# Tokens and gates in one product, and the two chunks of a group by turns in the halves of TensorE's columns, in a hybrid streaming encoder layer

## The chip, the cores and the metric

The kernel runs on one core of one Trainium2 chip. The metric is the device time of one execution in microseconds. The profile names the engines PE (matrix products), PEld (loads of the stationary operand, which overlap PE), DVE (vector), ACT (scalar), POOL and SP (which issues DMAs).

## What is computed

One inference step of one layer over 2048 prompt frames and 32 frames of a running stream. Three mixers work on parts of one input projection; the change touches the second and the third:

```python
hn = rmsnorm(x, norm1); proj = hn @ w_in
ya = rmsnorm(rg_lru(causal_conv(pa_x))) * gelu(pa_g)      # 256 channels
yb = rwkv7_mix(pb)                                        # 6 heads x 64, a recurrence over time
yc = mlstm_mix(pc)                                        # 6 heads x 64
# mlstm_mix, in chunks of 64 frames:
xact = silu(causal_conv(xc)); q = xact @ wq; k = xact @ wk
gates = concat([q, k, vc]) @ w_if + b_if                  # 12 columns: i_pre and logf of 6 heads
num = w_inter * (q @ C0) + (q @ k.T * exp(log_w - m)) @ v
h = num / max(|den|, exp(-m))
C_new = w0_end * C0 + (w_end * k).T @ v
# then
x = x + concat([ya, yb, yc]) @ w_out
x = x + (silu(g) * u) @ w_ffn_out                         # g, u = halves of rmsnorm(x) @ w_ffn_in
y = rmsnorm(x)
```

## The kernel before

The frames stand in four blocks of 512 (the last one 544, in two of 272, with the sample frames at its end). `inproj` makes the input projection of a block, `phase2` the output projection and the feed-forward part. Both use fp32r products of a high and a low part, 128x128 stationary by 512 or 272 columns, which the profile shows as writers of `pj`. The mixers run on groups of 128 frames, 16 of the prompt and one shorter group of the sample. A group has two chunks of 64 frames (`nch` is 2). Tiles named `rw` in the profile belong to the second mixer, tiles named `ml` to the third and the first.

Nothing is issued in the order in which the functions run. A recorder keeps every instruction with what it depends on. `order` then plays all engines forward with estimated durations (`cost`) and writes down an order for each engine: evacuations first, then weights, then mixers in bursts limited by a debt, and the `pj` products as filling (`Recorder.order`). Every instruction has the line of the recorder's call, L339, so tiles and shapes tell the groups apart. PE executes in the order written down, apart from what the hardware overlaps.

Four places matter.

`rwkv_c` ends with `yps`: for each chunk and each of three pairs of heads one product `Un,Hr` (stationary 128x64, 128 columns) and two products `SV,Fr` (stationary 128x64, 64 columns) that accumulate on it. Chunk 0 writes partitions 0 to 63, chunk 1 partitions 64 to 127, and thus the other half of the array's columns. All of chunk 0 is written ahead of chunk 1.

`mlstm` makes the gates `gp` by six products of `xa` and `v` with `wga` (128x128 by 12 columns), and later brings `v` and `k` to tokens by six transposes (`tokens`, into `vt` and `kt`, against the identity). `KW`, the weighted `k`, is read from PSUM by DVE.

`mlstm` makes its output `Op` by 12 products `R,QS` (128x64 by 65 columns), six for each chunk, chunk inside the loop. Those of chunk 0 need only the state at the group's start, those of chunk 1 the state `Rs[1]` after chunk 0.

`wq` and `wk` lie in SBUF for the whole time as a part of `smw`; the prompt groups don't read them.

Of the kernel before, what the change touches and what calls it, by code (L numbers as in the profile page):

```python
# [54 lines left out]
SMW = {}  # L55
# [7 lines left out]
NSMW = _n  # L63
NSMS = SMW["wif"][0]

# [80 lines left out]
class Op:  # L146
    __slots__ = ("eng", "fn", "args", "kw", "dur", "lat", "prio", "succ", "need", "ready", "start", "end", "idx", "rank", "mode")


class Recorder:  # L150
# [3 lines left out]
    def __init__(self, nc):  # L154
        self.ops = []
        self.level = MIX
        self.mem = {}
        self.masks = {}
        self.engines = {n: RecEngine(self, n, e) for n, e in (
            ("pe", nc.tensor), ("dve", nc.vector), ("act", nc.scalar), ("pool", nc.gpsimd), ("dma", nc.sync))}  # L160
# [41 lines left out]
    def add(self, eng, fn, name, args, kw):  # L202
# [13 lines left out]
        o.mode = tile_mode(ins[0]) if eng == "pe" else None  # L216
        deps = set()
        for a in ins:
# [28 lines left out]
    def order(self):  # L247
# [6 lines left out]
        debt, burst = 0.0, False  # L254
        mode = None
        for o in self.ops:
# [5 lines left out]
        while left:  # L262
# [36 lines left out]
            if best == "pe":  # L299
                if o.mode != mode:  # L300
                    when += DRAIN
                    mode = o.mode
                if o.prio == 1:
                    debt = max(debt, 0.0) + o.dur
                    burst = True
                elif o.prio == 2:
                    debt -= o.dur * RATE
                    burst = False
# [56 lines left out]
def cost(eng, name, out, ins, kw):  # L365

    n = 1
# [7 lines left out]
    if eng == "pe":  # L375
        if name == "transpose":
            return max(n, int(out.ap[0][1])) * 0.85, 196.0
        st = ins[0]
        if st.dtype == F32R:
            return max(n, 256) / 2.25 + 4.0, 196.0  # L380
        m = 1
        for _, c in list(st.ap)[1:]:
            m *= int(c)
        if m == 32:
            return max(38.0, 0.7 * n), 196.0
        if m == 64:
            return (92.0 if n < 70 else 1.15 * n), 196.0
        return 4.0 * max(m, n) / 2.4 + 4.0, 196.0
# [50 lines left out]
def hybrid_kernel(ctx, tc, A, O, cfg):  # L439
# [69 lines left out]

    wga = cp.tile([128, 6, 12], F32, name="wga")  # L510
    bones = cp.tile([128, 128], F32R, name="bones")
# [6 lines left out]
    histc = [cp.tile([128, 3, 3], F32, name=f"histc{i}") for i in range(2)]  # L518
    hlru = [cp.tile([128, 2], F32, name=f"hlru{i}") for i in range(2)]

    def setup():
# [26 lines left out]
        V.tensor_scalar(out=nsp, in0=nsp, scalar1=-4.0, scalar2=None, op0=ALU.mult)  # L548

        V.tensor_scalar(out=W("wq"), in0=W("wq"), scalar1=0.5, scalar2=None, op0=ALU.mult)  # L550
        V.tensor_scalar(out=W("wk"), in0=W("wk"), scalar1=0.5 / 8, scalar2=None, op0=ALU.mult)
        V.tensor_scalar(out=wif[:, 36:72], in0=wif[:, 36:72], scalar1=8.0, scalar2=None, op0=ALU.mult)


        V.tensor_copy(wga[:, 3:6, :], wif[:, 72:108].rearrange("p (a g) -> p a g", a=3))
        pg_ = mlp.tile([128, 512], F32, tag="ml", name="pg")
        wts = []
        for wn, o in (("wq", 0), ("wk", 36)):
            pt = rwp.tile([128, 512], F32, tag="rw", name="pt")[:, :384].rearrange("p (a t) -> p a t", a=3)
            for p in range(3):  # L560
                PE.transpose(pt[:, p, :], W(wn, 128 * p, 128 * p + 128), ident)
            wt = rws.tile([128, 3, 128], F32, tag="c" if o else "ta", name="wt")
            S.activation(wt, pt, AF.Copy)
            wts.append(wt)
            for p in range(3):
                PE.matmul(pg_[:, o + 12 * p:o + 12 * p + 12], wt[:, p, :], wif[:, o + 12 * p:o + 12 * p + 12], start=True, stop=True)
# [536 lines left out]
    def rwkv_c(Zf, BKU, SVt, UV, eL, g, bv, n_real, nch, st, col):  # L1103
# [53 lines left out]
        yps = rps("yps")[:, :384].rearrange("p (q t) -> p q t", q=6)  # L1157
        for c in range(nch):
            cs = slice(64 * c, 64 * c + 64)
            for p in range(3):  # L1160
                PE.matmul(yps[cs, 2 * p:2 * p + 2, :], Hr[:, p, c, 64:128], UN[c][:, p, :, :], start=True, stop=False)
                for j in range(2):
                    PE.matmul(yps[cs, 2 * p + j, :], Fr[:, p, c, 1, j, :], SVt[:, p, c, j, :],
                              start=False, stop=(j == 1))
# [37 lines left out]

    ml_state = [None, None]

    def mlstm_init(st):
# [16 lines left out]
    def mlstm_out(st, dst, dst_m):  # L1222
        R, mr = ml_state[st]
        if st == 0:
            ps = mps("mem")[:, :198].rearrange("p (a t) -> p a t", a=3)
            for p in range(3):
                for j, hs in halves():
                    PE.matmul(ps[hs, p, 0:65], W("wk", 128 * p + 64 * j, 128 * p + 64 * j + 64)[hs], R[hs, p, j, 0:65],
                              start=True, stop=True)
            for j, hs in halves():  # L1230
                S.activation(R[hs, :, j, 0:65], ps[hs, :, 0:65], AF.Copy)
        for j, hs in halves():
            SY.dma_start(dst[hs], R[hs, :, j, 0:65])
        SY.dma_start(dst_m, mr[:, 0:1])

    def mlstm(src, n_real, nch, st, col):
# [14 lines left out]
        k = t3("KW") if st else xa  # L1251
        for w_, dst in (((W("wq").rearrange("p (a e) -> p a e", a=3), None), (W("wk").rearrange("p (a e) -> p a e", a=3), k))
                        if st else ((wqk, None),)):
            ps = mps("qk")[:, :3 * n].rearrange("p (a t) -> p a t", a=3)
            for p in range(3):
                PE.matmul(ps[:, p, :], w_[:, p, :], xa[:, p, :], start=True, stop=True)
            if dst is not None:
                S.activation(dst, ps, AF.Copy)
            else:
                for j, hs in halves():  # L1260
                    S.activation(QM[hs, :, j, :n], ps[hs], AF.Copy)
        gp = mps("gp")
        for i_, x in enumerate((xa, v)):
            for p in range(3):
                PE.matmul(gp[:n, 0:12], x[:, p, :], wga[:, 3 * i_ + p, :], start=(i_ + p == 0), stop=(i_ + p == 3))
        gt = ml([128, 12], "gt")
        V.tensor_tensor(out=gt[:n], in0=gp[:n, 0:12], in1=bif[:n], op=ALU.add)
        f = gt[:n, 6:12]
# [7 lines left out]
        if n_real < n:  # L1276
# [13 lines left out]
                             op0=ALU.add, op1=ALU.max)  # L1290
        R, mr = ml_state[st]
        mu3 = mu.rearrange("p (c t) -> p c t", c=nch)
# [33 lines left out]
        for j, hs in halves():  # L1326
            oh = slice(64, 128) if j == 0 else slice(0, 64)
            S.activation(WI[hs], wl[oh], AF.Exp)
        QS = ml([128, 3, 2, 2, 64], "QS")[:, :, :nch]
        for j, hs in halves():  # L1330
# [4 lines left out]
            for c in range(nch):  # L1335
# [3 lines left out]
                            in1=ch(WI)[hs], op=ALU.mult)  # L1339
        D4 = ch(Dm)  # L1340
        W4 = ch(WI)
        Rs = [R]
        for c in range(nch):
            Rs.append(ml([128, 3, 2, 66], "R", bufs=3))
            G.memset(Rs[-1][:, :, :, 64:65], 1.0)
        vt = mps("vt")[:, :384].rearrange("p (a t) -> p a t", a=3)
        tokens(vt, v, n)
        for c in range(nch):
            for j in range(2):
                S.activation(Rs[c][64 * (1 - j):64 * (1 - j) + 64, :, j, 0:64],  # L1350
                             vt[64 * c:64 * c + 64, :, 64 * j:64 * j + 64], AF.Copy)
        kt = mps("kt")[:, :384].rearrange("p (a t) -> p a t", a=3)
        tokens(kt, k, n)
        KW = ml([128, 2, 3, 64], "KW")
        for c in range(nch):
            for j in range(2):
                oh = slice(64 * (1 - j), 64 * (1 - j) + 64)
                V.tensor_tensor(out=KW[oh, c], in0=kt[64 * c:64 * c + 64, :, 64 * j:64 * j + 64],
                                in1=bc(D4[oh, :, c, 63:64], [64, 3, 64]), op=ALU.mult)
        for c in range(nch):  # L1360
# [7 lines left out]
            for j, hs in halves():  # L1368
                V.tensor_tensor(out=Rn[hs, :, j, 0:65], in0=Rc[hs, :, j, 0:65],
                                in1=bc(W4[hs, :, c, 63:64], [64, 3, 65]), op=ALU.mult)  # L1370
                V.tensor_tensor(out=Rn[hs, :, j, 0:65], in0=Rn[hs, :, j, 0:65], in1=up[hs, :, 0:65], op=ALU.add)
        ml_state[st] = (Rs[nch], mr2)
        Op = mps("Op")[:, :396].rearrange("p (q t) -> p q t", q=6)
        for p in range(3):
            for j in range(2):
                for c in range(nch):
                    PE.matmul(Op[64 * c:64 * c + 64, 2 * p + j, 0:65], QS[:, p, c, j, :], Rs[c][:, p, j, 0:65],
                              start=True, stop=True)

        tm = mps("tm")  # L1380
# [314 lines left out]
```

## Time and profile before

| | |
|---|---|
| median of 3 runs | 2756.22 us (2750.87 to 2759.62) |
| profiled execution, its own time | 2758.22 us |
| its span in the profile | 2756.4 us |
| PE busy | 2699.3 us (98%) |
| DVE busy | 2170.4 us (79%) |
| ACT busy | 1290.2 us (47%) |
| mean granted clock of PE | 0.992 of full speed |

The profiled execution takes 1.8 us more than its span. A busy share is an average over the span; products overlap in PE's pipeline, so what a product costs is read from the start of one to the start of the next, not from its duration.

### The profile page before, as it was taken

To read this page: it belongs to the slowest core of one execution; us is meant where nothing else is said; L and a number is where in the kernel's file an instruction comes from. 1 tells how busy PE (TensorE), PEld (TensorE's weight loads), DVE (VectorE), ACT (ScalarE), POOL (GpSimd) and SP (SyncE) were. 2 spreads that over 40 slices of the span, in tenths; PEclk is the share of its full clock that TensorE was granted. 3 is DMA by queue.
4 is the path that set the end of the run, shared out by engine and by line. 5 is a ranking of instruction groups with operands and counts; after the bars stand their busy time and mean duration, and the time that the engine had idled before them with its cause. 6 is when DMAs were issued, how large, how long until landed. Compare 5 with 4: busy or idle time off the path is not lost.

```text
span 2756.4 us, 47320 instructions
## 1 busy us (share of the span) xinstructions
PE 2699.3 (98%) x17021; PEld 2324.8 (84%) x17021; DVE 2170.4 (79%) x6107; ACT 1290.2 (47%) x2847; POOL 44.3 (2%) x171
## 2 busy tenths in 40 slices
PE   8999999999999999999999999999999998999998
PEld 7888887999878888887888888788888888999997
DVE  6788879888897898979888898989888555545556
ACT  5565655656554454455444444644443333222223
POOL 0000000000000000000000000000000000000000
PEclk9999999999999999999999999999999999999999
DMA  6453543544433333344333333353333334232232
GB/s 240 144 173 116 175 139 119 166 128 119 126 89 101 97 92 110 88 124 153 98 107 97 105 95 105 105 161 98 85 99 89 96 110 147 85 93 85 85 93 79
DMA packets 235955, 317.86 MB, mean 115 GB/s; under 512 B 63848, under 2 KB 147736, under 8 KB 235592
## 3 DMA queue, kind: packets, MB, share of 16 engines
q1 hardware_dynamic: 189860, 300.74, 35.5%
q10 hardware_dynamic: 45860, 14.10, 2.4%
q8 instruction: 134, 2.20, 0.3%
q14 instruction: 101, 0.83, 0.1%
HBM read 268.50 MB, written 46.27 MB: 114 GB/s over the span
## 4 chain that ended last, share of the span: by engine, by line
PE 71%; DVE 20%; DMA 4%; ACT 3%; issue 2%; ACTq 0%; SPq 0%; DVEq 0%
PE pj L339 61%; PE rw L339 7%; DVE wl L339 4%; PE ml L339 4%; DVE stg L339 2%; DVE utmp L339 1%; DVE x L339 1%; DVE Z L339 1%; DVE al L339 1%; DVE hl L339 1%; DMA sq<-ymix 1%; DVE Fr L339 1%; ACT wh L339 1%; DVE Dm L339 1%; DVE acc L339 1%
## 5 line engine op out<-in xcount | busy, mean ns | idle before, releaser
L339 PE MATMUL pj<-ah,wh 128*128 128x512 f32 (+1 forms) x2560 | 894.2, 357 | 7.8 <-DVE x L339 6.5
L339 PE MATMUL pj<-al,wh 128*128 128x512 f32 (+1 forms) x2560 | 893.9, 356 | 0.2 <-DVE al L339 0.2
L339 PE MATMUL pj<-ah,wl 128*128 128x512 f32 (+1 forms) x2560 | 825.3, 354 | 1.0 <-DVE wl L339 1.0
L339 ACT ACTIVATE wh<-raw 128x1024 fp32r<-128x1024 f32 (+2 forms) x444 | 383.0, 863 | 735.3 <-PE pj L339 600.2
L339 PEld LDWEIGHTS pj<-ah,wh 128*128 128x128 f32 x2560 | 484.0, 189 | 73.0 <-DVE x L339 6.7
L339 PEld LDWEIGHTS pj<-al,wh 128*128 128x128 f32 x2560 | 486.7, 190 | 61.3 <-DVE al L339 0.8
L339 PEld LDWEIGHTS pj<-ah,wl 128*128 128x128 f32 x2560 | 454.2, 189 | 66.4 <-DVE wl L339 2.1
L339 DVE TENSOR_TENSOR wl<-raw,wh 128x1024 fp32r<-128x1024 f32 (+2 forms) x444 | 432.0, 974 | 62.3 <-ACT wh L339 61.0
L339 PE MATMUL pj<-hh,wh 128*128 128x512 f32 (+1 forms) x856 | 297.3, 359 | 3.4 <-ACT hh L339 3.4
L339 PE MATMUL pj<-hl,wh 128*128 128x512 f32 (+1 forms) x856 | 299.5, 357 | 0.4 <-DVE hl L339 0.4
L339 PE MATMUL pj<-hh,wl 128*128 128x512 f32 (+1 forms) x856 | 278.6, 355 | 0.0
L339 DVE TENSOR_TENSOR x<-x,pj 128x512 f32<-128x512 f32 (+1 forms) x280 | 158.5, 582 | 109.3 <-PE pj L339 102.3
L339 PEld LDWEIGHTS pj<-hh,wh 128*128 128x128 f32 x856 | 160.8, 189 | 27.0 <-ACT hh L339 4.8
L339 PEld LDWEIGHTS pj<-hl,wh 128*128 128x128 f32 x856 | 161.9, 190 | 24.1 <-DVE hl L339 3.3
L339 PE MATMUL pj<-ah,hh 128*128 128x512 f32 (+1 forms) x480 | 168.0, 357 | 7.5 <-ACT hh L339 7.4
L339 PEld LDWEIGHTS pj<-hh,wl 128*128 128x128 f32 x856 | 152.5, 189 | 22.3
L339 PE MATMUL pj<-al,hh 128*128 128x512 f32 (+1 forms) x480 | 168.2, 358 | 0.0
L339 PE MATMUL pj<-ah,hl 128*128 128x512 f32 (+1 forms) x480 | 154.4, 354 | 0.0
L339 DVE TENSOR_TENSOR cbuf<-pj,acc 128x512 f32<-128x512 f32 (+1 forms) x110 | 62.5, 585 | 87.0 <-PE pj L339 85.3
L339 DVE TENSOR_TENSOR stg<-stg,pj 128x512 f32<-128x512 f32 (+1 forms) x110 | 62.4, 583 | 85.6 <-PE pj L339 84.7
L339 DVE TENSOR_TENSOR utmp<-Z,BK 96x60 f32<-96x60 f32 (+27 forms) x527 | 106.1, 201 | 9.9 <-DMA BK<-tb 5.1
L339 DVE TENSOR_TENSOR Z<-Z,utmp 96x60 f32<-96x60 f32 (+27 forms) x527 | 106.1, 201 | 4.9
(343 smaller groups left out, 3896.8 us busy)
## 6 DMA issues: line engine op xcount, KB each, us to landing
raw<-in_w_ffn_in SPq DMA_DIRECT2D x176, 512.0 KB
raw<-in_w_ffn_out SPq DMA_DIRECT2D x128, 256.0 KB
raw<-in_w_in SPq DMA_DIRECT2D x96, 256.0 KB
raw<-in_w_in SPq DMA_DIRECT2D x48, 512.0 KB
spill<-stg SPq DMA_DIRECT2D x72, 256.0 KB
raw<-in_w_out SPq DMA_DIRECT2D x32, 512.0 KB
x<-in_xT SPq DMA_DIRECT2D x48, 256.0 KB
raw<-in_w_ffn_out SPq DMA_DIRECT2D x64, 192.0 KB
```

Source lines behind the costliest of these rows:

```text
L339: o.fn(*o.args, **o.kw)
```

## The change

Four edits. (1) In `yps` the loop over chunks goes inside, so that products of the two chunks alternate. (2) The gates and the tokens come out of one product: the new constant `iwg` holds, for each of six 128-row parts, the identity (128 columns) and beside it the part's gate weights (12 columns). `vt` and `kt` have 140 columns for each pair of heads; two reductions over the three parts and two additions make the gates; ACT copies the tokens of `k` to SBUF (`ks`), from which DVE makes `KW`. (3) All 12 products of `Op` wait in the order for the state after chunk 0 (`gate`). (4) The estimates that make the order change: a product with 64 stationary columns counts 4 + 0.85 ns a column, and one behind a product in the other half of the columns counts 7 ns. To make room for `iwg`, `wq` and `wk` are loaded twice, once in the setup and once ahead of the sample group.

```diff
@@ order
                 if o.mode != mode:
                     when += DRAIN
-                    mode = o.mode
+                    mode, side_ = o.mode, None
+
+                if mode[1] == 64 and side_ not in (None, o.col):
+                    o.dur = 7.0
+                    side_ = None
+                else:
+                    side_ = o.col
@@ cost
         if m == 64:
-            return (92.0 if n < 70 else 1.15 * n), 196.0
+            return 4.0 + 0.85 * n, 196.0
@@ constants and setup
-    wga = cp.tile([128, 6, 12], F32, name="wga")
+    iwg = cp.tile([128, 6, 140], F32, name="iwg")
+    wga = iwg[:, :, 128:140]
+    def load_qk(t):
+        o = SMW["wq"][0]
+        SY.dma_start(t, A["smalls"][:, o:o + 768])
+        V.tensor_scalar(out=t[:, 0:384], in0=t[:, 0:384], scalar1=0.5, scalar2=None, op0=ALU.mult)
+        V.tensor_scalar(out=t[:, 384:768], in0=t[:, 384:768], scalar1=0.5 / 8, scalar2=None, op0=ALU.mult)
+        S.activation(iwg[:, :, 0:128], bc(ident[:, None, :], [128, 6, 128]), AF.Copy)
@@ rwkv_c
-        for c in range(nch):
-            cs = slice(64 * c, 64 * c + 64)
-            for p in range(3):
-                PE.matmul(yps[cs, 2 * p:2 * p + 2, :], Hr[:, p, c, 64:128], UN[c][:, p, :, :], start=True, stop=False)
-                for j in range(2):
-                    PE.matmul(yps[cs, 2 * p + j, :], Fr[:, p, c, 1, j, :], SVt[:, p, c, j, :],
+        for p in range(3):
+            for c in range(nch):
+                PE.matmul(yps[64 * c:64 * c + 64, 2 * p:2 * p + 2, :], Hr[:, p, c, 64:128], UN[c][:, p, :, :],
+                          start=True, stop=False)
+            for j in range(2):
+                for c in range(nch):
+                    PE.matmul(yps[64 * c:64 * c + 64, 2 * p + j, :], Fr[:, p, c, 1, j, :], SVt[:, p, c, j, :],
                               start=False, stop=(j == 1))
@@ mlstm_out (ahead of the sample group)
+            wqk2[0] = ml([128, 768], "QS")
+            load_qk(wqk2[0])
@@ mlstm
-        gp = mps("gp")
-        for i_, x in enumerate((xa, v)):
-            for p in range(3):
-                PE.matmul(gp[:n, 0:12], x[:, p, :], wga[:, 3 * i_ + p, :], start=(i_ + p == 0), stop=(i_ + p == 3))
-        gt = ml([128, 12], "gt")
-        V.tensor_tensor(out=gt[:n], in0=gp[:n, 0:12], in1=bif[:n], op=ALU.add)
+        gt, ga = [ml([128, 12], f"gt{i}") for i in range(2)]
+        vt = mps("vt")[:, :420].rearrange("p (a t) -> p a t", a=3)
+        for p in range(3):
+            PE.matmul(vt[:n, p, :], v[:, p, :], iwg[:, 3 + p, :], start=True, stop=True)
+        V.tensor_reduce(out=gt[:n], in_=vt[:n, :, 128:140].rearrange("p a g -> p g a"), axis=AX.X, op=ALU.add)
+        V.tensor_tensor(out=gt[:n], in0=gt[:n], in1=bif[:n], op=ALU.add)
...
+        kt = mps("kt")[:, :420].rearrange("p (a t) -> p a t", a=3)
+        for p in range(3):
+            PE.matmul(kt[:n, p, :], xa[:, p, :], iwg[:, p, :], start=True, stop=True)
+        V.tensor_reduce(out=ga[:n], in_=kt[:n, :, 128:140].rearrange("p a g -> p g a"), axis=AX.X, op=ALU.add)
+        V.tensor_tensor(out=gt[:n], in0=gt[:n], in1=ga[:n], op=ALU.add)
...
+        S.activation(ks[:n], kt[:n, :, 0:128].rearrange("p a (j t) -> p a j t", j=2), AF.Copy)
...
-        vt = mps("vt")[:, :384].rearrange("p (a t) -> p a t", a=3)
-        tokens(vt, v, n)
...
-        kt = mps("kt")[:, :384].rearrange("p (a t) -> p a t", a=3)
-        tokens(kt, k, n)
...
-                V.tensor_tensor(out=KW[oh, c], in0=kt[64 * c:64 * c + 64, :, 64 * j:64 * j + 64],
+                    V.tensor_tensor(out=KW[oh, c], in0=ks[64 * c:64 * c + 64, :, j, :],
...
+            if c < nch - 1:
+                gate = len(rec.ops) - 1
+        rec.gate = gate if nch > 1 else None
         Op = mps("Op")[:, :396].rearrange("p (q t) -> p q t", q=6)
```

How the change moves instructions is shown on PE at three places. The first is `yps` of the first group: `Un0` and `Un1` are chunks 0 and 1. First before, then after.

```order
L339 MATMUL rw_0_170<-Un0_0_120,Hr_0_130 64x128
L339 MATMUL rw_0_170<-SV_0_155,Fr_0_129 64x64 x2
L339 MATMUL rw_0_170<-Un0_0_120,Hr_0_130 64x128
L339 MATMUL rw_0_170<-SV_0_155,Fr_0_129 64x64 x2
L339 MATMUL rw_0_170<-Un0_0_120,Hr_0_130 64x128
L339 MATMUL rw_0_170<-SV_0_155,Fr_0_129 64x64 x2
L339 MATMUL rw_0_170<-Un1_0_121,Hr_0_130 64x128
L339 MATMUL rw_0_170<-SV_0_155,Fr_0_129 64x64 x2
```

```order
L347 MATMUL rw_1_172<-UV_0_244,Fr_0_129 128x128 x3
L347 MATMUL rw_0_171<-Un0_0_120,Hr_0_130 64x128
L347 MATMUL rw_0_171<-Un1_0_121,Hr_0_130 64x128
L347 MATMUL rw_0_171<-SV_0_155,Fr_0_129 64x64 x4
L347 MATMUL rw_0_171<-Un0_0_120,Hr_0_130 64x128
L347 MATMUL rw_0_171<-Un1_0_121,Hr_0_130 64x128
```

The two chunks' products, nine in a row for each before, now stand by turns.

The second place is `Op` of the second group. `R_2_224` is the state at its start (chunk 0) and `R_0_222` the state after chunk 0; in the changed kernel these are `R_2_225` and `R_0_223`. Before, three products of chunk 0 are issued 37 rows earlier, in a block of their own, and the other nine stand here:

```order
L339 MATMUL pj_0_203<-ah6_0_190,hl1_0_144 128x512
L339 MATMUL ml_1_169<-R_2_224,QS_0_277 64x65
L339 MATMUL ml_1_169<-R_0_222,QS_0_277 64x65
L339 MATMUL ml_1_169<-R_2_224,QS_0_277 64x65
L339 MATMUL ml_1_169<-R_0_222,QS_0_277 64x65
L339 MATMUL ml_1_169<-R_2_224,QS_0_277 64x65
L339 MATMUL ml_1_169<-R_0_222,QS_0_277 64x65 x4
L339 MATMUL pj_0_203<-ah7_0_192,hh1_0_143 128x512
```

After the change (the first eight of the twelve):

```order
L347 MATMUL rw_0_171<-BK_0_168 64x64 x6
L347 MATMUL ml_0_169<-R_0_223,KW_0_279 64x65 x6
L347 MATMUL ml_1_170<-R_2_225,QS_0_267 64x65
L347 MATMUL ml_1_170<-R_0_223,QS_0_267 64x65
L347 MATMUL ml_1_170<-R_2_225,QS_0_267 64x65
L347 MATMUL ml_1_170<-R_0_223,QS_0_267 64x65
L347 MATMUL ml_1_170<-R_2_225,QS_0_267 64x65
L347 MATMUL ml_1_170<-R_0_223,QS_0_267 64x65
L347 MATMUL ml_1_170<-R_2_225,QS_0_267 64x65
L347 MATMUL ml_1_170<-R_0_223,QS_0_267 64x65
```

All twelve now stand in one block by turns. Over the whole program `Op` stands in 39 blocks before and in 19 after, for 17 groups.

The third place is the gates of the second group. Before:

```order
L339 MATMUL rw_0_170<-cl_0_128,bones_0_81 128x384
L339 MATMUL ml_0_168<-xi_0_264,wqk_0_82 128x128 x3
L339 MATMUL ml_1_169<-wga_0_80,xi_0_264 128x12 x5
L339 MATMUL rw_1_171<-cst_0_75,BK_0_241 128x128 x3
L339 MATMUL pj_0_203<-al7_0_193,hh1_0_143 128x512
```

After the change:

```order
L347 MATMUL rw_1_172<-yx_0_175,smw_0_77 128x128 x3
L347 MATMUL ml_1_170<-xi_0_264,wqk_0_82 128x128 x3
L347 MATMUL ml_0_169<-iwg_0_80,xi_0_264 128x140 x3
L347 MATMUL pj_2_206<-al1_0_179,hh2_0_151 128x512
L347 MATMUL pj_2_206<-ah1_0_178,hl2_0_152 128x512
```

Three products of 140 columns (those of `v`) stand where five of the six gate products were; the three of `xa` follow 20 rows later. The six transposes, which before stood further on, are gone.

## Rows read from the trace of the kernel before

**Rows 1.** Page, part 1: busy us, share of the span and instructions of each engine.
```profile
PE 2699.3 (98%) x17021; PEld 2324.8 (84%) x17021; DVE 2170.4 (79%) x6107; ACT 1290.2 (47%) x2847; POOL 44.3 (2%) x171
```

**Rows 2.** Windows: length, busy and count of PE, PEld, DVE, ACT, POOL, PEclk, DMA share, GB/s.
```profile
300.00:2100.00 1800.00, 1774.81 (x11069) 1489.16 (x11068) 1567.62 (x4701) 911.16 (x2109) 36.33 (x132) 0.99 0.38 113
2300.00:2500.00 200.00, 197.80 (x1559) 197.37 (x1560) 101.52 (x202) 58.56 (x92) 0.00 (x0) 0.99 0.30 95
```

**Rows 3.** Timeline of PE around one `yps`: start, us, engine, line, operation, count.
```profile
235.19 0.83 PE L339 MATMUL rw<-UV,Fr 128*128 128x128 f32 x6
235.95 0.43 PE L339 MATMUL rw<-Un,Hr 128*64 128x128 f32 x2
...
236.45 0.39 PE L339 MATMUL rw<-Un,Hr 128*64 128x128 f32 x2
...
236.90 0.38 PE L339 MATMUL rw<-Un,Hr 128*64 128x128 f32 x2
237.12 0.22 PE L339 MATMUL rw<-SV,Fr 128*64 128x64 f32 x1
237.13 0.32 PE L339 MATMUL rw<-Un,Hr 128*64 128x128 f32 x1
237.18 0.28 PE L339 MATMUL rw<-SV,Fr 128*64 128x64 f32 x2
237.29 0.27 PE L339 MATMUL rw<-Un,Hr 128*64 128x128 f32 x1
...
238.62 0.50 PE L339 MATMUL pj<-al,hh 128*128 128x512 f32 x1
238.96 0.40 PE L339 MATMUL pj<-ah,hl 128*128 128x512 f32 x1
239.19 0.39 PE L339 MATMUL pj<-ah,wh 128*128 128x512 f32 x1
```

**Rows 4.** Timeline of PE around the two blocks of one `Op`.
```profile
325.06 0.56 PE L339 MATMUL ml<-R,QS 128*64 128x65 f32 x6
325.56 0.50 PE L339 MATMUL pj<-ah,wh 128*128 128x512 f32 x1
...
335.50 0.40 PE L339 MATMUL pj<-ah,hl 128*128 128x512 f32 x1
335.82 0.92 PE L339 MATMUL ml<-R,QS 128*64 128x65 f32 x18
336.67 0.50 PE L339 MATMUL pj<-ah,hh 128*128 128x512 f32 x1
337.01 0.40 PE L339 MATMUL pj<-al,hh 128*128 128x512 f32 x1
```

**Rows 5.** Timeline of PE around one set of six transposes, one of six gate products.
```profile
1008.07 0.82 PE L339 MATMUL ml<-cst,xi 128*128 128x128 f32 x6
1008.64 0.47 PE L339 MATMUL pj<-hl,wh 128*128 128x512 f32 x1
1008.96 0.39 PE L339 MATMUL pj<-hh,wl 128*128 128x512 f32 x1
...
1071.83 0.83 PE L339 MATMUL ml<-xi,wqk 128*128 128x128 f32 x6
1072.50 1.41 PE L339 MATMUL ml<-wga,xi 128*128 128x12 f32 x12
1073.76 0.48 PE L339 MATMUL pj<-ah,wh 128*128 128x512 f32 x1
```

**Rows 6.** Groups of DVE and ACT by form: count, busy us, mean ns, idle before.
```profile
L339 DVE TENSOR_TENSOR gt<-ml,bif 128x12 f32<-128x12 f32 x16 | 2.7, 168 | 1.9 <-PE ml L339 1.6
L339 DVE TENSOR_REDUCE hmDm<-ml 128x6 f32<-128x384 f32 x16 | 8.8, 548 | 0.1
L339 ACT ACTIVATE g<-rw 128x384 f32<-128x384 f32 x16 | 7.8, 489 | 17.0 <-PE rw L339 6.7 <-DMA out_yT<-x 5.5 <-DMA BK<-tb 4.2
```

**Rows 7.** The chain that ended last, in time: start, us, what.
```profile
136.32 5.23 DMA xi<-spill
```

More of the change, by code (lines that the diff above doesn't have):

```diff
@@ L63 @@
 NSMW = _n
-NSMS = SMW["wif"][0]
+NSMS = SMW["wq"][0]
 def make_consts():
@@ L146 @@
 class Op:
-    __slots__ = ("eng", "fn", "args", "kw", "dur", "lat", "prio", "succ", "need", "ready", "start", "end", "idx", "rank", "mode")
+    __slots__ = ("eng", "fn", "args", "kw", "dur", "lat", "prio", "succ", "need", "ready", "start", "end", "idx", "rank", "mode", "col")
 class Recorder:
@@ L158, in __init__ @@
         self.masks = {}
+        self.gate = None
         self.engines = {n: RecEngine(self, n, e) for n, e in (
@@ L216, in add @@
         o.mode = tile_mode(ins[0]) if eng == "pe" else None
-        deps = set()
+        o.col = self.region(out)[1] if eng == "pe" else None
+        deps = set() if self.gate is None else {self.gate}
         for a in ins:
@@ L254, in order @@
         debt, burst = 0.0, False
-        mode = None
+        mode, side_ = None, None
         for o in self.ops:
@@ L548, in setup @@
         V.tensor_scalar(out=nsp, in0=nsp, scalar1=-4.0, scalar2=None, op0=ALU.mult)
-        V.tensor_scalar(out=W("wq"), in0=W("wq"), scalar1=0.5, scalar2=None, op0=ALU.mult)
-        V.tensor_scalar(out=W("wk"), in0=W("wk"), scalar1=0.5 / 8, scalar2=None, op0=ALU.mult)
+        wqk_ = rws.tile([128, 1024], F32, tag="BK", name="wqk_")[:, :768]
+        load_qk(wqk_)
         V.tensor_scalar(out=wif[:, 36:72], in0=wif[:, 36:72], scalar1=8.0, scalar2=None, op0=ALU.mult)
+        S.activation(iwg[:, :, 0:128], bc(ident[:, None, :], [128, 6, 128]), AF.Copy)
         V.tensor_copy(wga[:, 3:6, :], wif[:, 72:108].rearrange("p (a g) -> p a g", a=3))
@@ L557, in setup @@
         wts = []
-        for wn, o in (("wq", 0), ("wk", 36)):
+        for wn, o in ((0, 0), (384, 36)):
             pt = rwp.tile([128, 512], F32, tag="rw", name="pt")[:, :384].rearrange("p (a t) -> p a t", a=3)
             for p in range(3):
-                PE.transpose(pt[:, p, :], W(wn, 128 * p, 128 * p + 128), ident)
+                PE.transpose(pt[:, p, :], wqk_[:, wn + 128 * p:wn + 128 * p + 128], ident)
             wt = rws.tile([128, 3, 128], F32, tag="c" if o else "ta", name="wt")
@@ L1203, in hybrid_kernel @@
     ml_state = [None, None]
+    wqk2 = [None]
     def mlstm_init(st):
@@ L1227, in mlstm_out @@
                 for j, hs in halves():
-                    PE.matmul(ps[hs, p, 0:65], W("wk", 128 * p + 64 * j, 128 * p + 64 * j + 64)[hs], R[hs, p, j, 0:65],
+                    PE.matmul(ps[hs, p, 0:65], wqk2[0][hs, 384 + 128 * p + 64 * j:384 + 128 * p + 64 * j + 64], R[hs, p, j, 0:65],
                               start=True, stop=True)
@@ L1251, in mlstm @@
         k = t3("KW") if st else xa
-        for w_, dst in (((W("wq").rearrange("p (a e) -> p a e", a=3), None), (W("wk").rearrange("p (a e) -> p a e", a=3), k))
+        for w_, dst in (((wqk2[0][:, 0:384].rearrange("p (a e) -> p a e", a=3), None),
+                         (wqk2[0][:, 384:768].rearrange("p (a e) -> p a e", a=3), k))
                         if st else ((wqk, None),)):
@@ L1261, in mlstm @@
                     S.activation(QM[hs, :, j, :n], ps[hs], AF.Copy)
-        gp = mps("gp")
-        for i_, x in enumerate((xa, v)):
-            for p in range(3):
-                PE.matmul(gp[:n, 0:12], x[:, p, :], wga[:, 3 * i_ + p, :], start=(i_ + p == 0), stop=(i_ + p == 3))
-        gt = ml([128, 12], "gt")
-        V.tensor_tensor(out=gt[:n], in0=gp[:n, 0:12], in1=bif[:n], op=ALU.add)
+        R, mr = ml_state[st]
+        Rs = [R]
+        for c in range(nch):
+            Rs.append(ml([128, 3, 2, 66], "R", bufs=3))
+            G.memset(Rs[-1][:, :, :, 64:65], 1.0)
+        gt, ga = [ml([128, 12], f"gt{i}") for i in range(2)]
[4 more added lines that the diff above has]
+        V.tensor_tensor(out=gt[:n], in0=gt[:n], in1=bif[:n], op=ALU.add)
+        for c in range(nch):
+            for j in range(2):
+                S.activation(Rs[c][64 * (1 - j):64 * (1 - j) + 64, :, j, 0:64],
+                             vt[64 * c:64 * c + 64, :, 64 * j:64 * j + 64], AF.Copy)
+        kt = mps("kt")[:, :420].rearrange("p (a t) -> p a t", a=3)
[3 more added lines that the diff above has]
+        V.tensor_tensor(out=gt[:n], in0=gt[:n], in1=ga[:n], op=ALU.add)
+        if st:
+            kt = mps("kt")[:, :384].rearrange("p (a t) -> p a t", a=3)
+            tokens(kt, k, n)
+        ks = ml([128, 3, 2, 2, 64], "QS")
+        ks = (ks[:, :, 1] if st else ks.rearrange("p a c j t -> p (a c j t)")[:, :384].rearrange(
+            "p (a j t) -> p a j t", a=3, j=2))
+        S.activation(ks[:n], kt[:n, :, 0:128].rearrange("p a (j t) -> p a j t", j=2), AF.Copy)
         f = gt[:n, 6:12]
@@ L1290, in mlstm @@
                              op0=ALU.add, op1=ALU.max)
-        R, mr = ml_state[st]
         mu3 = mu.rearrange("p (c t) -> p c t", c=nch)
@@ L1328, in mlstm, with weigh @@
             S.activation(WI[hs], wl[oh], AF.Exp)
+        D4 = ch(Dm)
+        W4 = ch(WI)
+        KW = ml([128, 2, 3, 64], "KW")
+        def weigh():
+            for c in range(nch):
+                for j in range(2):
+                    oh = slice(64 * (1 - j), 64 * (1 - j) + 64)
+                    V.tensor_tensor(out=KW[oh, c], in0=ks[64 * c:64 * c + 64, :, j, :],
+                                    in1=bc(D4[oh, :, c, 63:64], [64, 3, 64]), op=ALU.mult)
+        if not st:
+            weigh()
         QS = ml([128, 3, 2, 2, 64], "QS")[:, :, :nch]
@@ L1339, in mlstm @@
                             in1=ch(WI)[hs], op=ALU.mult)
[L1340 to L1345, printed above, removed]
-        vt = mps("vt")[:, :384].rearrange("p (a t) -> p a t", a=3)
-        tokens(vt, v, n)
[L1348 to L1351, printed above, removed]
-        kt = mps("kt")[:, :384].rearrange("p (a t) -> p a t", a=3)
-        tokens(kt, k, n)
[L1354 to L1357, printed above, removed]
-                V.tensor_tensor(out=KW[oh, c], in0=kt[64 * c:64 * c + 64, :, 64 * j:64 * j + 64],
-                                in1=bc(D4[oh, :, c, 63:64], [64, 3, 64]), op=ALU.mult)
+        if st:
+            weigh()
         for c in range(nch):
@@ L1378, in mlstm @@
                               start=True, stop=True)
+        rec.gate = None
         tm = mps("tm")
```

## The prediction

> **What bounds the kernel now.** I read the page's part 1 first: PE is busy 2699.3 of 2756.4 us, DVE 2170.4, ACT 1290.2 [rows 1]. A busy PE alone says little, since products overlap in its pipeline. So I took the windows next. In the stretch in which mixers run beside the big products (300 to 2100 us) PE is idle for 1800.0 - 1774.8 = 25 us, DVE for 1800.0 - 1567.6 = 232 us, ACT for half of it, and the granted clock is 0.99. After the mixers (2300 to 2500) PE is idle for 2.2 us in 200 [rows 2]. The reader is to see that one engine is short of time nearly everywhere, at its full 2.4 GHz, and that DVE, at 87%, is next. The queue of `pj` products is never empty: in the order written down a whole `phase2` and part of another still stand behind the last mixer product, before and after the change. So a nanosecond that PE doesn't spend on a mixer product goes to a `pj` product, and the end comes earlier by as much, as long as DVE keeps up.
>
> What a product costs PE is then the time from its start to the next start, which the timeline of PE gives. A `pj` product of 512 columns takes 0.23 us (238.96 to 239.19) [rows 3]. An fp32 product shows as two records, two passes; a pass with 128 stationary rows and columns and 128 columns takes (1072.50 - 1071.83)/6 = 0.112 us [rows 5].
>
> **yps.** Before, it runs from 235.95 to 238.62, 2.67 us. One pair of heads of one chunk takes 236.90 - 236.45 = 0.45 us: two passes of `Un,Hr` at 0.11 and four of `SV,Fr` at 0.058 [rows 3]. That makes six times 0.45 for two chunks. Do two passes in different halves of the columns run at once? Two places show it. At the seam of the chunks, the only spot where neighbours lie in different halves, the first pass of chunk 1's `Un,Hr` starts at 237.13, 0.01 us behind a pass of chunk 0 and ahead of three passes of it that come earlier in the order (237.18 and after) [rows 3]. And the second block of an `Op`, 18 records whose first six products alternate, takes 336.67 - 335.82 = 0.85 us, where the first block, six records all of one chunk, takes 325.56 - 325.06 = 0.50 [rows 4]. With 0.058 a pass, six singles leave 0.50 - 0.35 = 0.15 for the change of tile mode; then 0.85 - 0.15 = 0.70 is 12 slots: six pairs and six singles. So a pair costs what one pass costs. After the change `yps` is three times (two pairs at 0.11, four pairs at 0.058) = 1.36 us, with 0.14 for the mode 1.50. Saved: 1.17 a group, 16 groups: **18.7 us** (the sample group has one chunk). Lower bound 0, if alternating products with 128 columns did not pair as those with 65 do; upper bound half of the 2.67, 21 us.
>
> The Trainium skill, "TensorE: Matmul & The Clock Gate", section "Part 3: Packing small matmuls", says matmuls keep strict program order. With two passes in one half behind each other, each pair would then begin one pass late; I get 0.52 instead of 0.45 us for a pair of heads, and 15 us instead of 18.7. The seam in this trace shows a pass started ahead of three earlier ones, so I keep 18.7. The same section says that a weight load overlaps running products only if it goes to other rows of the array; here both halves use all 128 rows. By that the alternating products would gain little, which is a rival below; the 0.85 us of the 18 records speak against it.
>
> **Op.** Most groups issue it in two blocks, 0.50 + 0.85 = 1.35 us [rows 4]. In one block by turns it is 12 slots, 0.85: 0.50 saved. One group already stands in one block, so 15 times, 7.5 us. A block also costs at its edges: 335.50 plus 0.23 is 335.73, but the block starts at 335.82 (0.09 late), and the `pj` product behind it takes 0.34 instead of 0.23 until the next start (0.11) [rows 4]. The order has 39 blocks before and 19 after: 20 times 0.20 is 4.0 us. Together **11.5 us**; lower bound 4 (edges alone), upper 13. The gate itself delays nothing that matters: products of chunk 0 wait for the state after chunk 0, which those of chunk 1 waited for anyway, and behind them on PE stand `pj` products that others can go ahead of in the written order.
>
> **Gates and tokens.** Six gate products take 1073.76 - 1072.50 = 1.26 us, and 0.09 more at the `pj` product behind (0.32 instead of 0.23, as at 1008.64); six transposes take 0.57 + 0.09 = 0.66 [rows 5]. Together 2.01. A gate pass with 12 columns costs as much as one with 128, 0.112, so the 12 columns were nearly all waste. Passes of 140 columns are not in the trace. Bound from below: 0.112 again, from above by the ratio of columns 0.112 x 140/128 = 0.122. A pass of 128 columns on 64 stationary columns takes 0.11 as well [rows 3], half the weight load at the same time, so columns set it: I take 0.122. Twelve passes: 1.46. Saved 0.55, 16 times: **8.8 us** (bounds 8.8 and 10.7).
>
> **What is added elsewhere.** DVE gets two reductions and two additions for one addition a group. An addition is 0.17 us; no reduction of 36 numbers is there, so 0.17 to 0.55 (one of 384 columns) [rows 6]; I take 0.17, since the columns fall by ten. That is 0.5 us a group, 8 us in all, in DVE's 232 us of idle time. ACT gets a copy of 384 columns, 0.49 us a group [rows 6], on an engine that is idle half the time. Neither is on PE's path by itself. But the mixers must keep pace: with 38 us less PE time in that stretch DVE's idle time falls from 232 to some 186 us. If PE's waits there grow in that ratio, 25 x 232/186 = 31: **6 us given back**. From below 0, from above the case below in which DVE decides. The second load of `wq` and `wk` is 384 KB, and the sample group's products wait for it; a larger load (576 KB) took 5.2 us on the chain [rows 7]. Weight loads behind it on SP come later by at most that, once. PE has filling left, so I count 0, at most 5. The extra copy and load of the setup lie beside DVE and ACT work that starts before the first mixer product; 0, at most 1.
>
> **Sum.** 18.7 + 11.5 + 8.8 = 39.0 saved, 6 given back: 33 us. The profiled execution took 2758.2 us for its span of 2756.4, so it would become 2725. It stands 2 us above the median of the three runs; for the median I say **2723 us**. A difference under 0.3% (8 us) is no difference that a measurement here can tell.
>
> **The rivals.**
> - *All of it, or more.* PE's waits don't grow, and the order happens to be kinder: it has 37 changes of tile mode fewer (310 to 273), 17 blocks' edges at most besides those of `Op`, of which few are counted above. 2756 - 39 = 2717, less 3 for edges, 2714; with fewer waits down to 2703. For it: a single DVE instruction of 0.17 us is small against a group's time (16 groups in some 1800 us). Chance 0.20.
> - *DVE eats half.* DVE at 87% loses pace, PE's waits for it double more than once. 2738 to 2742. For it: its idle time shrinks by a fifth; against: PE's waits now are 25 us in 1800. Chance 0.13.
> - *The halves don't pair with full rows* (the skill's rule on weight loads as a mechanism here: the load of one half's weights holds back until the other half's product is through). `yps` stays at 2.67, `Op` keeps its edges (4.0), gates 8.8, less 2 given back: 2756 - 11 = 2745. Against: the 12 slots above. Chance 0.04.
> - *DVE is the bound already*: its 232 us of idle time are unavoidable waits for others, and its 8 us more come on top: 2764, the same within the 0.3%. It would decide if PE's waits were short only because both run at the same pace; PE's 25 us against DVE's 232 speak against it. Chance 0.06.
> - *Slower: the written order misjudges PE.* The whole order is made anew with products that count 59 and 7 ns where two passes each run 117 ns a pair. PE then does more late than the order thinks, and where PE stands waiting in order for a mixer operand, no `pj` product can pass. The place is PE's waits, 57 us over the span [rows 1]. If they doubled: -39 + 57 = +18, 2774. It decides from 47 us of added waits, nearly 3 us a group. Against: a PE later than planned finds its operands ready sooner. Chance 0.05.
>
> **How the numbers follow.** The forecast, 2712 to 2734 by itself, has 0.52. With the rivals that ends on 1.00. The range leaves out the last three rivals and the lower tail of the first: 2706 to 2744. Faster by over 0.3%: 0.52 + 0.20 + 0.13 and most of the fourth case's 0.04, 0.88. Within 0.3%: 0.07. Slower: 0.05.
>
> **What would show it right or wrong.** In the timeline of PE: a `yps` of 1.5 us (2.67 if the halves don't pair, 1.7 in strict order); one `Op` block of 24 records in 0.85; 12 passes of 140 columns in 1.4 to 1.5, no transposes of `xi` in prompt groups. In the windows: PE idle between 300 and the mixers' end about 30 us; more than 60 means that DVE or the order took it. DVE's busy time up by about 8 us. The clock at 0.99; the prediction is wrong if it falls in the mixers' stretch.

## The result and the profile after

| | before | changed |
|---|---|---|
| median of 4 runs, one chip | 2755.24 us | 2719.14 us (2718.69 to 2720.29) |
| ratio, 95% interval | | 0.9868 (0.9855 to 0.9881) |
| span of the profiled execution | 2756.4 us | 2717.2 us |
| PE busy; span less PE busy | 2699.3; 57.1 | 2660.1; 57.1 |

The change saves 36 us, 1.3%; the forecast was 2723, and the time lies inside the range and inside the forecast's own. PE's busy time fell by 39.2 us, and its idle time is the same as before. The first part of the page for the changed kernel (answers to [rows 1]) and its window over the mixers' stretch (to [rows 2]):

```profile
PE 2660.1 (98%) x16922; PEld 2284.6 (84%) x16922; DVE 2178.1 (80%) x6160; ACT 1297.6 (48%) x2865; POOL 44.2 (2%) x171
```

```profile
300.00:2100.00 1800.00, 1775.80 (x11199) 1483.75 (x11199) 1615.61 (x4923) 932.00 (x2159) 36.33 (x133) 1.00 0.40 116
```

DVE is busy 7.7 us more in all; kernels here with the same DVE work in another order differ by up to 13 us in that total (2165.8 in e10, 2179.1 in e9), so what was added is read by form below. In the 1800 us it has 184 us of idle time left, where it had 232; PE has 24.2, where it had 25.2. The granted clock is 1.00 of full speed in this stretch, so PE stays at its 2.4 GHz.

The same `yps` as in [rows 3], in the timeline of PE of the changed kernel:

```profile
239.35 0.44 PE L347 MATMUL rw<-Un,Hr 128*64 128x128 f32 x4
239.62 0.40 PE L347 MATMUL rw<-SV,Fr 128*64 128x64 f32 x8
239.85 0.39 PE L347 MATMUL rw<-Un,Hr 128*64 128x128 f32 x4
...
240.52 0.40 PE L347 MATMUL rw<-SV,Fr 128*64 128x64 f32 x8
240.85 0.50 PE L347 MATMUL pj<-ah,hh 128*128 128x512 f32 x1
```

It lasts 240.85 - 239.35 = 1.50 us, as in 14 of the 16 prompt groups (the others have a wait inside, or run into another product of 64 stationary columns). A pair of heads now takes 0.45 us for both chunks, where it took 0.45 for one. An `Op` (to [rows 4]) and three of the six joint products (to [rows 5]) of the changed kernel, from the same view:

```profile
1031.93 0.92 PE L347 MATMUL ml<-R,QS 128*64 128x65 f32 x24
1032.78 0.33 PE L347 MATMUL ml<-cst,RWW 128*128 128x128 f32 x1
...
1094.97 0.88 PE L347 MATMUL ml<-iwg,xi 128*128 128x140 f32 x6
1095.60 0.48 PE L347 MATMUL pj<-hl,wh 128*128 128x512 f32 x1
1095.92 0.40 PE L347 MATMUL pj<-hh,wl 128*128 128x512 f32 x1
```

`Op` stands in one block of 24 records and takes 0.85 us, in each of the 16 groups. Three joint products take 0.63 us and cost the `pj` product behind them 0.09 (0.32 instead of 0.23): 0.72, so 1.44 for six, 0.12 a pass. (A pass is one of the two records of an fp32 product.) What the new instructions cost DVE and ACT (to [rows 6]), by form:

```profile
L347 DVE TENSOR_REDUCE gt<-ml 128x12 f32<-128x36 f32 x32 | 6.0, 189 | 11.4 <-PE ml L347 9.9 <-ACT R L347 0.7 <-ACT QS L347 0.7
L347 ACT ACTIVATE QS<-ml 128x384 f32<-128x384 f32 x16 | 8.0, 497 | 5.9 <-PE ml L347 5.2 <-DVE gt L347 0.6
```

### The profile page after: what moved, and what is told of

It is laid out like the page before. It is cut to its first block, busy times and chain, and to the rows that moved or that the text cites. A ratio compares the mean times of both kernels' runs of the same rounds, so it can differ in the third digit from the quotient of the medians.

```text
span 2717.2 us, 47168 instructions
## 1 busy us (share of the span) xinstructions
PE 2660.1 (98%) x16922; PEld 2284.6 (84%) x16922; DVE 2178.1 (80%) x6160; ACT 1297.6 (48%) x2865; POOL 44.2 (2%) x171
```

## The experiments

The first theory is that of the prediction: what is saved is PE time of products, and the parts add up. The rival is that the order, which every edit makes anew, made the gain. The ratios are each to the kernel before on the same chip, with 95% intervals; 0.001 is 2.75 us. PE idle is the span of the profiled execution less PE's busy time, from the page. A block is a run of one kind of product on PE with no other between; its edges are the time lost where it begins and ends. The tile mode is the shape of the stationary operand, and the order counts how often it changes.

| kernel | ratio (interval) | span | PE busy | PE idle |
|---|---|---|---|---|
| before | 1 | 2756.4 | 2699.3 | 57.1 |
| changed | 0.9868 (0.9855 to 0.9881) | 2717.2 | 2660.1 | 57.1 |
| e1, yps by chunk | 0.9936 (0.9921 to 0.9950) | 2734.7 | 2683.0 | 51.7 |
| e2, no gate | 0.9937 (0.9922 to 0.9952) | 2735.4 | 2672.2 | 63.2 |
| e3, gates and tokens apart | 0.9860 (0.9844 to 0.9877) | 2713.5 | 2659.4 | 54.1 |
| e4, before with new estimates | 0.9918 (0.9904 to 0.9933) | 2728.3 | 2685.6 | 42.7 |
| e5, before, slack 330 | 1.0006 (0.9997 to 1.0015) | 2755.8 | 2696.3 | 59.5 |
| e6, changed, slack 330 | 0.9884 (0.9869 to 0.9899) | 2717.4 | 2657.3 | 60.1 |
| e7, apart, slack 330 | 0.9926 (0.9911 to 0.9940) | 2733.0 | 2672.0 | 61.0 |
| e8, changed, old estimates | 1.0011 (1.0000 to 1.0021) | 2757.6 | 2671.9 | 85.7 |
| e9, estimates doubled | 0.9951 (0.9932 to 0.9970) | 2733.6 | 2667.7 | 65.9 |
| e10, estimates halved | 0.9835 (0.9820 to 0.9850) | 2707.9 | 2656.5 | 51.4 |
| e11, yps in blocks of three | 0.9892 (0.9877 to 0.9907) | 2721.0 | 2664.5 | 56.5 |
| e12, load on DVE | 0.9938 (0.9923 to 0.9953) | 2737.3 | 2668.7 | 68.6 |

**e1: yps by chunk again.** The edit goes back to the old loop:

```diff
-        for p in range(3):
-            for c in range(nch):
+        for c in range(nch):
+            cs = slice(64 * c, 64 * c + 64)
+            for p in range(3):
...
```

> The changed kernel with the loop over chunks outermost in yps again, all else as changed. Theory (what is saved is PE time of pairs, to be added up): yps back at 2.67 us a group, so 16 x 1.17 = 19 us more than the changed kernel, 2738 us. Rival (the new order of issue, not the pairing, made the gain): within 5 us of 2719.

0.9936 against 0.9868: 0.0068, 19 us, as the theory had it. PE's busy time rises by 22.9 us, and its idle time falls by 5.4. In its timeline `yps` is back at 2.67 us:

```profile
237.89 0.43 PE L347 MATMUL rw<-Un,Hr 128*64 128x128 f32 x2
...
240.56 0.50 PE L347 MATMUL pj<-ah,hh 128*128 128x512 f32 x1
```

Added up from start to start over all groups, idle time left out, `yps` takes 44.3 us here and 25.5 in the changed kernel. What follows: in PE time the pairs in `yps` are worth the 18.7 us that were counted for them. That the whole time moves by the same 19 us is the outcome of one order.

**e2: no gate.**

```diff
-        rec.gate = gate if nch > 1 else None
+        rec.gate = None
```

> The changed kernel without the gate on Op: its 12 products stand in 38 blocks instead of 19. Theory: pairs lost (7.5 us) and 19 more block edges at 0.20 us (4 us), 11 us more, 2730. Rival (the order alone made the gain; here too an order is made anew): within 5 us of 2719.

0.0069, 19 us, more than the 11 expected. PE's busy time rises by 12.1 us, which is the expected part; its idle time rises by 6.1 on top. Of the 12.1, 8.6 are in `Op` itself and 3.5 in the `pj` products, whose time holds the edges. So the gate is worth its pairs and edges in PE time; the rest is waits of an order made anew.

**e3: gates and tokens apart.** The kernel before with the loops of `yps`, the gate and the estimates of the change, without `iwg`:

```diff
-        gp = mps("gp")
...
+            PE.matmul(vt[:n, p, :], v[:, p, :], iwg[:, 3 + p, :], start=True, stop=True)
```

These are some of the lines of the change that this run leaves out.

> The kernel before with three of the four edits (yps by turns, gate on Op, new estimates), gates and tokens made as before by six products and six transposes. Theory: 16 x 0.57 = 9 us more than the changed kernel, 2728. Rival (the joint product gives nothing, since its extra work on DVE and ACT costs as much): 2719 or below.

A miss: 0.9860, not slower than the changed kernel within the intervals, though its six products and six transposes cost PE 2.01 us a group where the joint ones cost 1.44. Its PE idles 3.0 us less, and PE's busy time is 0.7 us less in spite of the dearer products, so elsewhere on PE some 9 us were saved: 5.1 in the `pj` products and 4.0 in mixer products that no edit touched. Taken alone this run speaks for the rival.

**e4: the estimates alone.** The kernel before with edit (4) and nothing else:

```diff
-            return (92.0 if n < 70 else 1.15 * n), 196.0
+            return 4.0 + 0.85 * n, 196.0
...
```

> The kernel before with only the estimates of the order changed, no product moved by hand. Op stands in 33 blocks instead of 39, changes of tile mode fall from 310 to 273. Theory: only the edges, 18 round trips at 0.34 us, and few pairs: 2746 to 2755. Rival (the order made the gain): 2730 or below.

0.9918, 23 us faster, with every product as before. The median, 2731, is 1 us above the rival's bound and 15 below the theory's. PE idles 14.4 us less and is busy 13.7 us less, and the latter lies in mixer products that none of the edits moves (303.9 to 290.0 us). So the order alone can move the time by as much as `yps` did, and the parts can't be read from one order each.

**e5, e6, e7: chance of the order.** Three kernels with one estimate changed that says nothing of products:

```diff
-SLACK = 300.0
+SLACK = 330.0
```

> The kernel before with one estimate of the order changed that says nothing of products: the slack added to what a mixer instruction waits for, 330 instead of 300 ns. Every instruction stays, the order is made anew (282 changes of tile mode instead of 310, Op in 38 blocks). Theory A (the 21 us of the estimates alone are chance of the order): this one too moves by 8 us or more, to either side, by stalls of PE and edges, with yps and Op as before. Theory B (the new estimates of products are better): it stays within 5 us of 2752.

> The changed kernel with the slack at 330 instead of 300 ns. Theory A: it moves by up to 10 us about 2719, yps 25, Op 15 and gates with tokens 22 us stay. Theory B: within 5 us of 2719.

> The kernel with gates and tokens apart (three of the four edits) with the slack at 330 instead of 300 ns. Theory A (its lead of 5 us over the changed kernel is chance of the order, the joint product is worth 8 us of PE): it ends slower than the changed kernel with the same slack, by some 8 us, or by chance up to 10 us off that. Rival (the joint product costs more than it saves, by what it adds to DVE and ACT): it is again faster by some 5 us.

The kernel before doesn't move (1.0006), so the 8 us of theory A don't come there; the changed one moves by 0.0016, within the intervals; the one with gates and tokens apart loses 0.0066, 18 us, 12.6 of them in PE's busy time and 6.9 in its idle time. With this slack the joint product leads by 0.0042, 12 us; with the other the two are level. So what the joint product is worth in time isn't settled by these four: between nothing and 12 us, where the rows show 9 us of PE time.

**e8: the changed kernel with the old estimates.**

```diff
-            return 4.0 + 0.85 * n, 196.0
+            return (92.0 if n < 70 else 1.15 * n), 196.0
...
-                if mode[1] == 64 and side_ not in (None, o.col):
-                    o.dur = 7.0
...
```

> The changed kernel with the old estimates: products moved, gate, joint product, but 64-column products count 92 or 147 ns. Theory A: the moved work is worth 35 us of PE by itself, so 2715 to 2730. Theory B (the new estimates make 21 us of the gain): 2740.

1.0011, outside of both theories: with pairs, gate and joint products but an order by the old estimates, the whole gain is gone. PE's busy time is 27.4 us under that of before; its idle time is 28.6 us over it. The waits of PE, first of the changed kernel, then of e8 (engine, tile waited for; us in total, times, longest):

```profile
PE pj L347 <- ACT hh L347: 11.1, 7, 6.5
...
PE ml L347 <- DVE QS L347: 4.1, 5, 1.2
...
PE rw L347 <- DVE Fr L347: 2.3, 4, 0.9
...
PE ml L347 <- DVE wl L347: 1.4, 2, 1.1
PE rw L347 <- DVE yx L347: 1.2, 3, 0.6
```

```profile
PE ml L342 <- DVE QS L342: 8.9, 11, 2.0
...
PE rw L342 <- DVE yx L342: 7.6, 5, 1.8
PE rw L342 <- DVE Fr L342: 6.3, 8, 1.2
PE ml L342 <- DVE WI L342: 5.1, 6, 3.3
PE rw L342 <- DVE UV L342: 3.5, 5, 1.0
```

Most of the added waits are those of mixer products for DVE: 41.2 us in e8, 19.9 in the changed kernel, 18.6 before. One of them in the timeline of e8:

```profile
607.16 0.29 PE L342 MATMUL pj<-al,hh 128*128 128x272 f32 x1
607.82 0.46 PE L342 MATMUL rw<-Fr,BK 128*128 128x128 f32 x2 [0.37 <-DVE Fr L342]
610.06 0.55 PE L342 MATMUL rw<-cst,yx 128*128 128x128 f32 x3 [1.78 <-DVE yx L342]
```

Two mixer products stand one behind the other without a `pj` product between, and PE waits 1.78 us for the second. The old estimates count a pair of 65 columns at 184 ns, where the trace shows 0.12 us. So the order would believe that PE reaches the second product later than it does, and that DVE is done by then. That is argued from the estimates; what times the order had for these two products is not shown.

That makes a second theory, C: an order that counts PE's products too long makes PE wait, one that counts them too short doesn't. (In the kernel before, where most of these products stand alone, even the old estimates are too short: 92 ns for one of 65 columns, whose two passes take 0.116 us. So e4, which shortens them further, is no case of "too long".)

**e9 and e10: the estimates doubled and halved.**

```diff
-            return 4.0 + 0.85 * n, 196.0
+            return 8.0 + 1.7 * n, 196.0
```

The halved kernel has `2.0 + 0.425 * n` in this place.

> The changed kernel with its estimate of a product with 64 stationary columns doubled (8 + 1.7 ns a column, the second of a pair still 7), which is what two passes take in the trace: a pair at 0.12 us. Theory C (an order that counts PE too long makes PE wait, one that counts it too short costs nothing): estimates that are true cost little, 2715 to 2727, stalls 50 to 65 us; the loss of e8 comes from singles at 92 and 147 ns that count a pair at 184 and 294. Theory A (chance of the order): anywhere within 2710 to 2740.

> The changed kernel with that estimate halved (2 + 0.425 ns a column), four times too short against the trace. Theory C: stalls of PE no more than in the changed kernel (56 us), 2700 to 2722. Theory A: 2710 to 2740. Third: an order that is false in either direction loses, 2730 or more.

Halved: 0.9835, faster than the changed kernel beyond both intervals, 2708.0 us, the fastest of all; that is inside theory C's range, 2 us outside theory A's, and speaks against the third. Doubled: 0.9951, 2738.5 us, slower, outside of what theory C expected of true durations and inside theory A's range. From the halved estimate to the changed one, the doubled and the old one PE's idle time goes 51.4, 57.1, 65.9, 85.7 us and its busy time 2656.5, 2660.1, 2667.7, 2671.9. So the direction of C holds in these four and in e4 against before; that true durations cost little doesn't. Each is one order, and e7 shows that one can be off by 18 us by chance. The page of e10, part 1:

```profile
PE 2656.5 (98%) x16922; PEld 2283.9 (84%) x16922; DVE 2165.8 (80%) x6160; ACT 1293.4 (48%) x2865; POOL 43.9 (2%) x171
```

**e11: yps in blocks of three.** The second loop over chunks is taken out, so that three products of a chunk (six passes) follow each other:

```diff
             for c in range(nch):
                 PE.matmul(yps[64 * c:64 * c + 64, 2 * p:2 * p + 2, :], Hr[:, p, c, 64:128], UN[c][:, p, :, :],
                           start=True, stop=False)
-            for j in range(2):
-                for c in range(nch):
+                for j in range(2):
```

> The changed kernel with yps by turns of three products instead of one: for each pair of heads chunk 0's Un,Hr and two SV,Fr (six passes), then chunk 1's. How far ahead PE takes passes: at the seam of the kernel before, 0.17 us of nine products overlapped. By that five seams give 5 x 0.17 us, yps 2.0 us, 16 x 0.5 = 8 us more than the changed kernel, 2727. Rival 1 (PE reaches as far as six passes): 1.5 us, 2719. Rival 2 (only direct neighbours overlap): 2.6 us, 2737.

The timeline of PE of this kernel around one `yps`:

```profile
1634.33 0.43 PE L347 MATMUL rw<-Un,Hr 128*64 128x128 f32 x2
1634.60 0.22 PE L347 MATMUL rw<-SV,Fr 128*64 128x64 f32 x1
1634.61 0.32 PE L347 MATMUL rw<-Un,Hr 128*64 128x128 f32 x1
1634.66 0.28 PE L347 MATMUL rw<-SV,Fr 128*64 128x64 f32 x2
...
1636.30 0.50 PE L347 MATMUL pj<-al,wh 128*128 128x512 f32 x1
```

1.97 us, as expected from the seam, in place of 1.50; over all groups `yps` takes 7.2 us more PE time. The ratio is 0.0024 (7 us) above the changed kernel's, in the direction expected, but the intervals touch. The second `Un,Hr` (chunk 1) starts at 1634.61, after one of four `SV,Fr` passes of chunk 0 that the order puts ahead of it. So PE starts a pass ahead of some three earlier ones of the other half, and not of six; of the two spacings tried, only partners next to each other overlap fully.

**e12: a load on DVE.**

```diff
+        for _ in range(4):
+            V.tensor_reduce(out=spin, in_=iwg[:, :, 0:128], axis=AX.X, op=ALU.add)
         f = gt[:n, 6:12]
```

> The changed kernel with four reductions of 768 columns a group on DVE that nothing needs, some 3.5 us a group, 59 us in all, known to the order. DVE's idle time in the mixers' stretch falls from 184 to some 125 us. If PE's waits grow as DVE's idle time shrinks: 24 x 184/125, 11 us more, 2730. If DVE has room: 2719 to 2722. If DVE already sets the pace: 2760 or more.

The load as traced (count; shortest, median and longest in ns; first and last start in us), and this kernel's window over the mixers' stretch (to [rows 2]):

```profile
L347 DVE TENSOR_REDUCE spin<-iwg x68: 914/948/956, 26.8 to 204.1; 128x6 f32<-128x768 f32 x68
```

```profile
300.00:2100.00 1800.00, 1769.93 (x11175) 1480.12 (x11173) 1597.56 (x4863) 935.91 (x2174) 36.49 (x133) 1.00 0.38 116
```

The edit didn't make the condition that the expectation speaks of. The reductions read only a constant, so they wait for nothing, and the order put all 68 of them between 26.8 and 204.1 us, not four beside each group. In the 1800 us DVE is idle for 202 us, more than the 184 of the changed kernel, not 125. PE's idle time does rise by 11.5 us, where 11 were expected, but 5.5 of them are in the first 300 us and 5.9 in the mixers' stretch: the match is chance. What the run shows is that 64.5 us of DVE work ahead of the mixers went with a first `yps` 37 us later (276.8 against 239.4) and a time 19 us longer (0.0070), in one order, in which PE's busy time rises by 8.6 us too. How much room DVE has beside the mixers is not shown.

## Why the prediction was right

The forecast of 2723 us came out 4 us above the 2719 that were measured, and what it said of the single products holds. How the parts add up holds in part by luck. PE's time, each product from its start to the next one's start, summed over the trace, idle time left out, in us (gates and tokens of the prompt groups):

| | before | e4, estimates alone | e8, products alone | changed |
|---|---|---|---|---|
| `yps` | 44.3 | 44.3 | 26.1 | 25.5 |
| `Op` | 23.0 | 22.4 | 17.4 | 14.7 |
| gates and tokens | 31.0 | 30.6 | 21.4 | 20.7 |
| other mixer products | 303.9 | 290.0 | 304.9 | 297.6 |
| `pj` | 2297.1 | 2298.3 | 2302.1 | 2301.5 |
| idle | 57.1 | 42.7 | 85.7 | 57.1 |

- *yps, 18.7 us.* 1.50 us was forecast and is there; the table has 18.8, and e1 gives it back. Pairs of products with 128 columns behave as those with 65 do.
- *Op, 11.5 us.* One block of 0.85 us in every prompt group, as forecast; 8.3 us in the table, where 7.5 were counted for the pairs. The 4.0 us for its edges can't be told apart in the change, since the new order spreads the `pj` products over more blocks (366 instead of 310 in the trace) and they take 4.5 us more; e2, where less else moves, shows 3.5.
- *Gates and tokens, 8.8 us.* 1.44 us a group against the forecast 1.46, so 9 us of PE time. That this is worth 9 us of time is not shown: e3 says nothing, e7 says 12.
- *DVE and ACT.* 8 us more on DVE were forecast; by form two reductions and one more addition make 8.6. A reduction takes 0.189 us (0.17 was taken), the copy 0.497 (0.49).
- *39.0 saved on PE.* PE's busy time fell by 39.2, but the moved products give 37.4 of it; 6.3 come from the other mixer products, most of which no edit touches, and the `pj` products take 4.5 back. The near match of the two sums is luck.
- *6 us given back* is the term that was mis-sized: "If PE's waits there grow in that ratio, 25 x 232/186 = 31: 6 us given back". PE idles 24.2 us there. It was the wrong thing to scale, because the estimates changed with the work. With the same estimates the moved products bring more idle time than 6: 28.6 us with the old ones (before to e8), 14.4 with the new ones (e4 to changed). The new estimates by themselves take 14.4 away (before to e4). (In the 1800 us of the mixers' stretch alone the three are 27.4, 10.5 and 11.5.) That the two cancel to 0 was not foreseen. No run shows the ratio by itself, since e12 didn't change DVE's idle time as meant.
- *The rival "All of it, or more"* has the balance that came: idle time as before, and a span that is shorter by what PE's busy time lost, 2756.4 - 39.2 = 2717.2, where the forecast had 6 us given back. It names a kinder order, and e4 shows one.
- *The rival "the written order misjudges PE"* had its place and kind right, and its "Against" names the direction that e8 then showed: "a PE later than planned finds its operands ready sooner". Its size was the largest unknown of the case. Edit (4) looked like bookkeeping in the prediction, counted by fewer edges alone. Of the 36 us, 23 came with the estimates alone (e4), and the three other edits add 14 to them (0.9918 to 0.9868); without the estimates they add nothing (e8). Each of these is one order.
- *The rule on weight loads*: the Trainium skill, "TensorE: Matmul & The Clock Gate", section "Part 3: Packing small matmuls", says that loads overlap running products only towards other rows. As the mechanism of the rival in the prediction it would have left `yps` at 2.67 us; the trace shows 1.50 with both halves on all 128 rows. The same section's strict program order gives 1.7 us for the changed `yps`, an estimate of the prediction; 1.50 was measured, and e11 shows passes ahead of their order.

Open: why one order is 18 us better than another with the same work and nearly the same estimates (e3 and e7), beyond the fact that PE's edges and its waits for DVE both differ; and which part of the gain is a property of the estimates and which is chance of the orders they happened to give.

## What to carry to other kernels

Where one engine is short of time and a queue of filling stands behind it, price an edit by start-to-start times in that engine's own timeline, with the edges of a mode change; in a single group the products came out within a few per cent here. What that time is worth at the end depends on the waits that the new order brings, and those were not forecast. Two fp32 products with 64 stationary columns cost one here (`yps` 1.50 us instead of 2.67) when they went to different halves of the columns and stood next to each other in program order. Where an order is computed from estimated durations, a change of the work and a change of its estimates are one edit: test each with the other left out, and perturb an estimate that should not matter, before reading a difference under 1% as the worth of an edit. When a load is added to test an engine's room, look in the trace where it ran (e12).

## What the runs showed of the hardware

PE starts a pass of one half of the columns ahead of earlier passes of the other half: by some three passes of 0.058 us, not by six (e11, and the seam in [rows 3]). An fp32 pass of 140 columns takes 0.12 us, against 0.112 for 128 or for 12. With the same instructions in another order (e8 against the changed kernel) PE was idle for 28.6 us more, 21 of them in waits of mixer products for DVE that last about 1 us each.
